# Attention's softmax sums divided out at the gate, and five element-wise steps moved between engines, in a two-layer hybrid diffusion step

## The chip, the cores and the metric

One core of a Trainium2 chip runs the whole step as one program. The metric is the device time of one execution in microseconds (us). Engines are named as in the profile: PE is TensorE's matmul (PEld its weight loads), DVE is VectorE, ACT is ScalarE, POOL is GpSimd, SP is the engine that issues most transfers.

## The reference

The model is a backbone of two layers over 640 tokens (512 latent, 128 context) of 1024 channels, in float32. Each layer normalises the tokens, projects them to 76 blocks of 128 columns (and 48 more), runs four branches on column slices of that, and merges the branches:

- RWKV-7 time mixing, in both directions, 8 heads handled as 4 pairs; at the end a group norm, a bonus term and a gate
- multi-head latent attention, 8 heads of 64 value columns, latent tokens over 640 keys, context tokens over 128
- a Mamba-2 state space branch (SSD)
- an RG-LRU: a gated linear recurrence, in both directions

The part that the change is about most is the attention, where the output is also multiplied by a gate afterwards:

```python
s = jnp.einsum('bqhd,bkhd->bhqk', qblk, k).astype(F32) * scale
p = jax.nn.softmax(s, axis=-1).astype(v.dtype)
return jnp.einsum('bhqk,bkhd->bqhd', p, v)
...
branches = jnp.stack([o_rw * jax.nn.silu(rw_gate), o_mla * jax.nn.silu(mla_gate), ...
```

and of the RG-LRU: `u = sqrt(-expm1(2 log_a)) * (g_i * xc)`, then the scan `h = a h + u` forward and backward.

## The kernel before

Activations lie with channels on the 128 partitions and the 640 tokens in the free dimension. Dense projections (`dense`, `zs`, `merge`, `output`) split both operands into a rounded part and a remainder and make three matmuls of 320 columns from each product (L246); the weights are split by an ACT cast (L233) and a DVE subtraction (L234).

The program runs a layer in stages. RWKV comes first, with projections that later stages need as background. Then two generators are woven with a background queue at fixed rates: `mla_heads` and then `mla_attend` for the attention, `lru` for the RG-LRU, and the remaining dense projections. After that SSD runs beside the merge projections, then the output projection. Generators emit instructions; a planner then orders each engine's list when the program is built, taking emission order as priority and its own costs as time, so that an instruction may stand later in an engine's list than instructions emitted after it. Each engine works its list strictly in that order.

In `mla_attend` a unit is one head and one tile of 128 queries. For a unit, `scores` makes six matmuls into a PSUM pair of banks (`pd`, two buffers; L1181), DVE takes the maximum (L1184) and scales it (L1186), ACT makes the exponentials with their row sums (`ae`, L1188), DVE takes the reciprocal of the sums (L1189) and multiplies the exponentials by it (L1190). `turn_p` transposes the result on PE in blocks of 128 (L1199: five, or one for the context tile), and copies the five blocks out of PSUM: four on ACT (L1201), the fifth on DVE (L1203), into `aPT`. The scores of the unit two later are emitted right after a unit's transposes. At a pair's second head (`e == 1`) a DVE operation on two columns (L1129) joins the two heads' copies, and the value products of both heads (L1132) go to one PSUM bank (`oT`, one buffer) that holds four token tiles; after the fourth tile and after the context tile, DVE multiplies them with the gate (L1136). Between them stand the transposes of the next heads' queries and keys (`turned`, L1081) with their splits (L1084, L1085, L239, L240).

In `lru`, for each of 4 blocks and 2 directions, DVE prepares the gates (L1458 to L1462), POOL multiplies (L1463), ACT takes a square root for both directions (L1468), POOL multiplies again (L1472), and DVE scans latent and context tokens (L1476). In `rw_end`, POOL makes the bonus term (L889) and, behind DVE's norm (L893, L894), adds it (L895); PE then transposes the sum (L541).

Of the kernel before, what the change touches and what calls it, by code (L numbers as in the profile page):

```python
# [10 lines left out]
F32 = mybir.dt.float32  # L11
# [10 lines left out]
TL, TC = 512, 128  # L22
# [147 lines left out]
class K:  # L170
# [703 lines left out]
    def rw_end(self, l, p, H, od):  # L874
# [17 lines left out]
        self.rsqrt(s2, s1, 1.0 / 64, 64e-5, p)  # L892
        tt(out=on, in0=on, in1=bc(s2), op=ALU.mult)  # L893
        tt(out=on, in0=on, in1=P["lng"][:, pr * 64:pr * 64 + 64].unsqueeze(1).broadcast_to([128, 10, 64]), op=ALU.mult)  # L894
        nc.gpsimd.tensor_tensor(out=on, in0=on, in1=q3, op=ALU.add)  # L895
        gate = p.tile([128, T], F32, name="gate", tag="rwv", bufs=1)
        nc.sync.dma_start(out=gate, in_=self.z(l, Z_RWG + pr))
        yield
# [159 lines left out]
    def mla_attend(self, l, od):  # L1058
# [37 lines left out]
        self.turn = {}  # L1096
        yield from heads((0, 1))
        todo = heads(range(2, 8))
        S = {}
        units = [(hp, t, e) for hp in range(4) for t in range(5) for e in range(2)]  # L1100
        keys = lambda t: range(5) if t < 4 else (5,)
        for i, u in enumerate(units[:2]):
            S[u] = self.scores(p, self.turn[u[2]], u[1])
            yield
        for i, (hp, t, e) in enumerate(units):
            if t == 0 and e == 0:
                gate = p.tile([128, T], F32, name="mg", tag="mg", bufs=1)
                nc.sync.dma_start(out=gate, in_=gd[hp])
            if t == 1 and e == 0:
                self.silu_sb(p, gate, "mo")  # L1110
                o32 = p.tile([128, T], F32, name="mo", tag="mo", bufs=1)
            S[hp, t, e] = self.turn_p(p, *S[hp, t, e], len(keys(t)))
            yield
            if i + 2 < len(units):
                n = units[i + 2]
                h = 2 * n[0] + n[2]
                while h not in self.turn:
                    next(todo)
                S[n] = self.scores(p, self.turn[h], n[1])
                yield  # L1120
            if next(todo, 1) is None:
                yield
            if e == 1:
                if t % 4 == 0:
                    oT = self.ps("o")
                o = oT[:, t % 4 * 128:t % 4 * 128 + 128]

                k = 511 if len(keys(t)) > 1 else 0
                nc.vector.scalar_tensor_tensor(out=S[hp, t, 0][:, 0:2], in0=S[hp, t, 1][:, k:k + 2], scalar=0.0, in1=S[hp, t, 0][:, 0:2], op0=ALU.mult, op1=ALU.add)  # L1129
                for j, kt in enumerate(keys(t)):  # L1130
                    for x in range(2):
                        nc.tensor.matmul(o[64 * x:64 * x + 64], vt[:, kt, hp * 128 + 64 * x:hp * 128 + 64 * x + 64],  # L1132
                                         S[hp, t, x][:, j * 128:j * 128 + 128], start=j == 0, stop=j == len(keys(t)) - 1)
                if t >= 3:
                    tok = slice(0, TL) if t == 3 else slice(TL, T)
                    nc.vector.tensor_tensor(out=o32[:, tok], in0=oT[:, 0:tok.stop - tok.start], in1=gate[:, tok], op=ALU.mult)  # L1136
                yield
                if t == 4:
                    nc.sync.dma_start(out=od[:, hp], in_=o32)
# [28 lines left out]
        nc.vector.tensor_tensor(out=x, in0=x, in1=cos, op=ALU.mult)  # L1168
        nc.vector.tensor_tensor(out=x, in0=x, in1=s, op=ALU.add)

    def scores(self, p, qk, t):

        nc = self.nc
        pd = self.pd()
# [11 lines left out]
        nc.vector.tensor_scalar(out=m[:, 0:1], in0=m[:, 0:1], scalar1=-scale, scalar2=None, op0=ALU.mult)  # L1186
        e = p.tile([128, 2, 320], F32, name="ae", tag="ae", bufs=2)[:, 0:len(cuts), 0:w]
        nc.scalar.activation(out=e, in_=view, func=AF.Exp, scale=scale, bias=m[:, 0:1], accum_out=m[:, 1:2])  # L1188
        nc.vector.reciprocal(out=m[:, 1:2], in_=m[:, 1:2])  # L1189
        nc.vector.tensor_scalar(out=e, in0=e, scalar1=m[:, 1:2], scalar2=None, op0=ALU.mult)  # L1190
        return pd, e

    def turn_p(self, p, pd, e, n):

        nc = self.nc
        e = e.rearrange("p a b -> p (a b)")
        PT = p.tile([128, T], F32, name="aPT", tag="aPT", bufs=3)
        for i in range(n):
            nc.tensor.transpose(pd[:, i // 4, i % 4 * 128:i % 4 * 128 + 128], e[:, i * 128:i * 128 + 128], self.c["ident"])  # L1199
        k = min(n, 4)  # L1200
        nc.scalar.copy(PT[:, 0:k * 128], pd[:, 0, 0:k * 128])  # L1201
        if n > 4:
            nc.vector.tensor_copy(PT[:, TL:T], pd[:, 1, 0:128])  # L1203
        return PT

    def conv(self, u, acc, w, b, taps):
# [200 lines left out]
    def lru(self, l, od):  # L1407
# [26 lines left out]
        for blk in range(4):  # L1434
# [6 lines left out]
            for d in range(2):  # L1441
# [18 lines left out]
                stt(out=e, in0=tr, scalar=2.0, in1=e, op0=ALU.add, op1=ALU.mult)  # L1460
                stt(out=tr, in0=t2, scalar=1.0, in1=e, op0=ALU.add, op1=ALU.mult)
                stt(out=ti, in0=ti, scalar=1.0, in1=xc, op0=ALU.add, op1=ALU.mult)  # L1462
                pt_(out=ti, in0=ti, in1=e, op=ALU.mult)  # L1463
                un.append((tr, ti, t2))
                if d == 0 and b < 4:
                    ahead = conved(*ahead)
# [2 lines left out]
            hs = []  # L1469
            for d, (tr, ti, t2) in enumerate(un):  # L1470
                i = 4 * d + blk
                pt_(out=t2, in0=t2, in1=ti, op=ALU.mult)  # L1472
                for t0, t1, init in ((0, TL, P["slru"][:, i:i + 1]), (TL, T, 0.0)):
                    s = slice(t0, t1)
                    rv = (lambda x: x[:, s]) if d == 0 else (lambda x: x[:, s][:, ::-1])
                    nc.vector.tensor_tensor_scan(rv(ti), rv(tr), rv(t2), init, ALU.mult, ALU.add)  # L1476
                nc.gpsimd.tensor_copy(fin[:, d, blk:blk + 1], ti[:, T - 1:T] if d == 0 else ti[:, TL:TL + 1])
                hs.append(ti)
                yield
# [262 lines left out]
```

## Time and profile before

| | |
|---|---|
| median of 3 runs | 2428.43 us (2424.76 to 2429.99) |
| profiled execution | 2425.01 us, its span 2423.1 us |
| PE busy | 2295.9 us, 95% |
| DVE busy | 1709.8 us, 71% |
| ACT busy | 1101.4 us, 45% |
| POOL busy | 485.1 us, 20% |
| mean granted TensorE clock | 0.974 |

A share of busy time is a mean over stages. The time of PE's records overlaps, as matmuls are pipelined, so the spacing of starts tells what one costs. The profile names for each idle stretch of an engine what ended it; the windows give busy times and the granted clock for a stretch; the timeline lists an engine's instructions in order of time.

### The profile page before, as it was taken

Reading aid. Unit: us, or ns where it says so; the run is one execution under the profiler, and the core shown is the slowest. Engines: PE = TensorE matmul, PEld = TensorE weight load, DVE = VectorE, ACT = ScalarE, POOL = GpSimd, SP = SyncE. Lnnn points to the kernel's source line nnn. Section 1 sums busy time; section 2 is a strip of 40 time slices with the busy share of each in tenths; the row PEclk is TensorE's granted clock in tenths of the full one; section 3 lists DMA queues with packets and bytes.
Section 4 is the critical chain, followed back from the end, with each engine's and each line's share of the span. In section 5 each row is a group of like instructions: output and inputs, shape, how many; then the busy total and the mean of one; then the engine's idle time right before and its main releaser. Section 6 shows DMA issues by size and latency. Waiting matters only on the chain. (4 is left out here: it accounts for less than half of the span.)

```text
span 2423.1 us, 52542 instructions
## 1 busy us (share of the span) xinstructions
PE 2295.9 (95%) x21106; PEld 2044.0 (84%) x21106; DVE 1709.8 (71%) x3831; ACT 1101.4 (45%) x2182; POOL 485.1 (20%) x645
## 2 busy tenths in 40 slices
PE   6999999999989999999999999999999988999999
PEld 4888778889988888987998979797989977898799
DVE  6684767665487878597766767777737877788973
ACT  3544344443345665562335353535224555656331
POOL 0211212231101120144012121213111013103520
PEclk9999999999999999999999999899999999999999
DMA  6553434423432213734633424141424322155354
GB/s 247 167 167 118 133 121 131 126 84 109 135 123 78 80 65 112 251 115 127 212 97 123 128 65 132 59 120 61 123 84 152 106 83 89 63 173 191 118 171 131
DMA packets 159204, 300.98 MB, mean 124 GB/s; under 512 B 59881, under 2 KB 70601, under 8 KB 158961
## 3 DMA queue, kind: packets, MB, share of 16 engines
q1 hardware_dynamic: 158528, 296.24, 37.7%
q8 instruction: 166, 2.72, 0.5%
q0 software_dynamic: 432, 1.38, 0.2%
q14 instruction: 78, 0.63, 0.1%
HBM read 221.17 MB, written 76.39 MB: 123 GB/s over the span
## 5 line engine op out<-in xcount | busy, mean ns | idle before, releaser
L246 PE MATMUL dn<-hh,whi 128*128 128x320 f32 x2368 | 765.3, 323 | 3.2 <-ACT zst L279 1.4
L246 PE MATMUL dn<-hl,whi 128*128 128x320 f32 x2368 | 745.4, 315 | 0.0
L246 PE MATMUL dn<-hh,wlo 128*128 128x320 f32 x2368 | 744.9, 315 | 0.0
L246 PEld LDWEIGHTS dn<-hh,whi 128*128 128x128 f32 x2368 | 447.8, 189 | 32.6 <-issue 6.8
L246 PEld LDWEIGHTS dn<-hl,whi 128*128 128x128 f32 x2368 | 448.7, 189 | 7.1 <-issue 1.8
L246 PEld LDWEIGHTS dn<-hh,wlo 128*128 128x128 f32 x2368 | 447.6, 189 | 6.5 <-issue 2.8
L234 DVE TENSOR_TENSOR wlo<-raw,whi 128x1024 fp32r<-128x1024 f32 (+1 forms) x184 | 240.6, 1308 | 122.3 <-ACT whi L233 119.2
L233 ACT CAST whi<-raw 128x1024 fp32r<-128x1024 f32 (+1 forms) x184 | 191.5, 1041 | 229.8 <-PE dn L246 194.9
L246 PE MATMUL dn<-omh,whi 128*128 128x320 f32 x408 | 135.7, 335 | 6.5 <-DVE mx L1541 2.9
L246 PE MATMUL dn<-oml,whi 128*128 128x320 f32 x408 | 131.4, 322 | 3.5 <-DVE oml L240 3.5
L810 POOL COPY S<-V 64x128 f32<-64x128 f32 x128 | 57.4, 448 | 382.6 <-PE ps L541 176.5
L246 PE MATMUL dn<-omh,wlo 128*128 128x320 f32 x408 | 129.2, 318 | 3.2 <-DVE wlo L234 3.2
L541 PE MATMUL ps<-Q,BK 64*64 64x192 f32 x1280 | 103.3, 342 | 13.7 <-DVE Q L673 11.2
L673 DVE TENSOR_TENSOR Q<-ps,cpack 64x384 f32<-64x384 f32 x160 | 88.8, 555 | 38.6 <-ACT W L671 34.4
L541 PEld LDWEIGHTS ps<-S,Q 128*64 128x64 f32 x1920 | 74.1, 143 | 36.1 <-issue 18.4
L281 ACT COPY zst<-dn 128x320 f32<-128x320 f32 (+1 forms) x104 | 43.9, 422 | 131.1 <-PE dn L246 90.9
L541 PE MATMUL ps<-S,Q 128*64 128x64 f32 x1920 | 90.4, 233 | 10.8 <-DVE S L855 6.5
L246 PEld LDWEIGHTS dn<-omh,whi 128*128 128x128 f32 x408 | 78.6, 194 | 25.4 <-issue 9.1
L671 ACT COPY W<-ps 64x384 f32<-64x384 f32 x160 | 75.6, 473 | 52.0 <-PE ps L541 49.5
L277 ACT ACTIVATE zst<-dn 128x320 f32<-128x320 f32 x128 | 55.5, 434 | 90.0 <-PE dn L246 60.6
L541 PEld LDWEIGHTS ps<-Q,BK 64*64 64x64 f32 x1280 | 60.3, 136 | 38.7 <-DVE Q L673 19.6
L756 DVE TENSOR_TENSOR X<-X,Lu 80x31 f32<-80x31 f32 (+15 forms) x248 | 85.5, 345 | 6.8 <-DMA X<-in_eye_dram 0.8
(575 smaller groups left out, 4837.2 us busy)
## 6 DMA issues: line engine op xcount, KB each, us to landing
raw<-in_w_in_dram SPq DMA_DIRECT2D x152, 512.0 KB
zd<-zst SPq DMA_DIRECT2D x150, 320.0 KB
raw<-in_ada_w_dram SPq DMA_DIRECT2D x48, 512.0 KB
th<-zd SPq DMA_DIRECT2D x64, 320.0 KB
raw<-in_w_branch_dram SPq DMA_DIRECT2D x32, 512.0 KB
om<-od SPq DMA_DIRECT2D x32, 320.0 KB
u<-zd SPq DMA_DIRECT2D x26, 320.0 KB
raw<-in_w_out_dram SPq DMA_DIRECT2D x16, 512.0 KB
```

The source lines that it names most:

```text
L233: nc.scalar.copy(hi[:, 0:w], raw[:, 0:w])
L234: nc.vector.tensor_tensor(out=lo[:, 0:w], in0=raw[:, 0:w], in1=hi[:, 0:w].bitcast(F32), op=ALU.subtract)
L246: self.nc.tensor.matmul(o, w[wi], x[xi][:, sl], start=first and i == 0, stop=last and i == 2)
L277: nc.scalar.activation(out=u[:, tok], in_=t, func=AF.Tanh, scale=0.5)
L281: nc.scalar.copy(u[:, tok], t)
L541: self.nc.tensor.matmul(o, x, y, start=start, stop=stop, skip_group_check=True)
L671: nc.scalar.copy(W[r, u:u + 2].rearrange("p u x t -> p (u x t)"), ps[e][r, 0:384])
L673: nc.vector.tensor_tensor(out=Q[e][o, u:u + 2].rearrange("p u x t -> p u (x t)"), in0=ps[e][o, 0:384].rearrange("p (u x) -> p u x", u=2), ...
L756: nc.vector.tensor_tensor(out=o, in0=X[0:nb, 0:m, k:k + 1].broadcast_to([nb, m, n]), in1=Lu[0:nb, k, k + 1:].unsqueeze(1).broadcast_to([nb ...
L810: nc.gpsimd.tensor_copy(S[e][o, 0:2], pairs(V[o], s))
```

## The change

In attention the exponentials are no longer multiplied by the reciprocal. The reciprocals of a pair's two heads are written to two columns of a small tile (`rs`). For each pair of units PE spreads them: one transpose of the second head's column, broadcast to 128 columns, ahead of the value products, and one of the first head's column, broadcast to 64, over the upper half behind them. They lie in the right half of the PSUM bank `oT`, which now holds two token tiles and is taken three times per head pair in place of twice. DVE multiplies the gate by the spread reciprocals and then the products by the gate, after tiles 1, 3 and 4. The copy out of `turn_p` is one ACT copy of all blocks, and the join of the two heads' copies is an ACT operation on one column in place of a DVE one on two.

In the RG-LRU the two POOL multiplies per block and direction are on DVE, and in `rw_end` the last sum is on DVE.

```diff
-        nc.gpsimd.tensor_tensor(out=on, in0=on, in1=q3, op=ALU.add)
+        tt(out=on, in0=on, in1=q3, op=ALU.add)
...
-        S = {}
+        S, r = {}, {}
...
-        for i, u in enumerate(units[:2]):
-            S[u] = self.scores(p, self.turn[u[2]], u[1])
+        def scores(hp, t, e):
+            if e == 0:
+                r[hp, t] = p.tile([128, 2], F32, name="rs", tag="ar", bufs=3)
+            S[hp, t, e] = self.scores(p, self.turn[2 * hp + e], t, r[hp, t][:, e:e + 1])
+
+        for u in units[:2]:
+            scores(*u)
...
             if e == 1:
-                if t % 4 == 0:
+                if t % 2 == 0:
                     oT = self.ps("o")
-                o = oT[:, t % 4 * 128:t % 4 * 128 + 128]
-                k = 511 if len(keys(t)) > 1 else 0
-                nc.vector.scalar_tensor_tensor(out=S[hp, t, 0][:, 0:2], in0=S[hp, t, 1][:, k:k + 2], scalar=0.0, in1=S[hp, t, 0][:, 0:2], op0=ALU.mult, op1=ALU.add)
+                o, ro = (oT[:, i + t % 2 * 128:i + t % 2 * 128 + 128] for i in (0, 256))
+                nc.tensor.transpose(ro, r[hp, t][:, 1:2].broadcast_to([128, 128]), c["ident"])
+                k = 639 if len(keys(t)) > 1 else 0
+                nc.scalar.activation(out=S[hp, t, 0][:, 0:1], in_=S[hp, t, 1][:, k:k + 1], func=AF.Identity, scale=0.0, bias=S[hp, t, 0][:, 0:1])
                 for j, kt in enumerate(keys(t)):
                     for x in range(2):
                         nc.tensor.matmul(o[64 * x:64 * x + 64], vt[:, kt, hp * 128 + 64 * x:hp * 128 + 64 * x + 64],
                                          S[hp, t, x][:, j * 128:j * 128 + 128], start=j == 0, stop=j == len(keys(t)) - 1)
-                if t >= 3:
-                    tok = slice(0, TL) if t == 3 else slice(TL, T)
-                    nc.vector.tensor_tensor(out=o32[:, tok], in0=oT[:, 0:tok.stop - tok.start], in1=gate[:, tok], op=ALU.mult)
+                nc.tensor.transpose(ro[0:64], r[hp, t][:, 0:1].broadcast_to([128, 64]), c["ident"])
+                if t % 2 or t == 4:
+                    n = 256 if t < 4 else 128
+                    tok = slice((t + 1) * 128 - n, (t + 1) * 128)
+                    nc.vector.tensor_tensor(out=gate[:, tok], in0=oT[:, 256:256 + n], in1=gate[:, tok], op=ALU.mult)
+                    nc.vector.tensor_tensor(out=o32[:, tok], in0=oT[:, 0:n], in1=gate[:, tok], op=ALU.mult)
...
-        nc.vector.reciprocal(out=m[:, 1:2], in_=m[:, 1:2])
-        nc.vector.tensor_scalar(out=e, in0=e, scalar1=m[:, 1:2], scalar2=None, op0=ALU.mult)
+        nc.vector.reciprocal(out=r, in_=m[:, 1:2])
...
-        k = min(n, 4)
-        nc.scalar.copy(PT[:, 0:k * 128], pd[:, 0, 0:k * 128])
-        if n > 4:
-            nc.vector.tensor_copy(PT[:, TL:T], pd[:, 1, 0:128])
+        nc.scalar.copy(PT[:, 0:n * 128], pd.rearrange("p a b -> p (a b)")[:, 0:n * 128])
...
-                pt_(out=ti, in0=ti, in1=e, op=ALU.mult)
+                tt(out=ti, in0=ti, in1=e, op=ALU.mult)
...
-                pt_(out=t2, in0=t2, in1=ti, op=ALU.mult)
+                tt(out=t2, in0=t2, in1=ti, op=ALU.mult)
```

## Rows read from the trace of the kernel before

**Rows 1.** The page's first part: engine, busy us, share of the span, instructions.
```profile
PE 2295.9 (95%) x21106; PEld 2044.0 (84%) x21106; DVE 1709.8 (71%) x3831; ACT 1101.4 (45%) x2182; POOL 485.1 (20%) x645
```

**Rows 2.** Windows, attention's stretches: length, then busy us by engine, granted clock, DMA.
```profile
780.00:980.00 200.00, 186.14 (x1371) 164.93 (x1370) 164.32 (x375) 124.70 (x241) 33.18 (x25) 0.97 0.29 92
...
1960.00:2172.00 212.00, 196.50 (x1428) 174.74 (x1428) 169.05 (x380) 128.27 (x247) 37.81 (x27) 0.96 0.29 95
```

**Rows 3.** PE's waits, whole span: who waited for whom, total us, times, longest us.
```profile
PE pd L1199 <- DVE ae L1190: 18.5, 11, 4.7
...
PE ps L1081 <- DVE qTl L1085: 6.7, 5, 2.1
...
PE ps L1132 <- DVE aPT L1129: 4.4, 2, 4.1
...
PE ps L541 <- POOL on L895: 2.0, 1, 2.0
```

**Rows 4.** Timeline of DVE: start us, us, instruction, idle time before it and its end.
```profile
862.15 2.59 DVE L1476 TENSOR_TENSOR_SCAN lt<-lt,pcol,l 128x512 f32<-128x512 f32 x1 [1.71 <-POOL l L1472]
...
2044.69 0.15 DVE L1186 TENSOR_SCALAR m<-m 128x1 f32<-128x1 f32 x1
2047.97 2.55 DVE L1476 TENSOR_TENSOR_SCAN lt<-lt,pcol,l 128x512 f32<-128x512 f32 x1 [3.12 <-POOL l L1472]
...
2050.76 1.25 DVE L1476 TENSOR_TENSOR_SCAN lt<-lt,pcol,l 128x512 f32<-128x512 f32 x1
...
2052.25 0.13 DVE L1189 RECIPROCAL m<-m 128x1 f32<-128x1 f32 x1
...
2093.41 2.57 DVE L1476 TENSOR_TENSOR_SCAN lt<-lt,pcol,l 128x512 f32<-128x512 f32 x1 [0.90 <-POOL l L1472]
```

**Rows 5.** Timeline of ACT, same stretch.
```profile
2047.53 0.80 ACT L1188 ACTIVATE ae<-pd,m 128x640 f32<-128x640 f32 x1
...
2048.31 0.58 ACT L1201 COPY aPT<-pd 128x512 f32<-128x512 f32 x1
```

**Rows 6.** Timeline of PE, same stretch.
```profile
2048.00 0.31 PE L246 MATMUL dn<-hl,whi 128*128 128x320 f32 x1
2048.14 0.31 PE L246 MATMUL dn<-hh,wlo 128*128 128x320 f32 x1
2053.12 0.87 PE L1199 MATMUL pd<-cpack,ae 128*128 128x128 f32 x3 [4.66 <-DVE ae L1190]
...
2054.05 0.47 PE L1181 MATMUL pd<-kTl,qTh 96*128 96x320 f32 x1
2054.32 0.47 PE L1181 MATMUL pd<-kTh,qTl 96*128 96x320 f32 x1
```

**Rows 7.** DVE's groups by line and form: count, busy us, mean ns, idle before.
```profile
L234 DVE TENSOR_TENSOR wlo<-raw,whi 128x1024 fp32r<-128x1024 f32 x182 | 239.5, 1316 | 121.3 <-ACT whi L233 118.2 <-ACT xs L833 1.9 <-DMA cv<-lx 0.4
...
L1190 DVE TENSOR_SCALAR ae<-ae,m 128x640 f32<-128x640 f32 x64 | 41.2, 644 | 1.1
...
L1203 DVE COPY aPT<-pd 128x128 f32<-128x128 f32 x64 | 18.1, 284 | 14.1 <-ACT aPT L1201 13.6
...
L1345 DVE TENSOR_TENSOR yo<-pd,ea 128x256 f32<-128x256 f32 x40 | 15.0, 410 | 1.9 <-PE pd L1341 1.9
...
L1544 DVE TENSOR_TENSOR y<-y,mx 128x640 f32<-128x640 f32 x16 | 13.1, 819 | 0.1
```

**Rows 8.** Timeline of PE at five transposes of the SSD stage.
```profile
1021.00 0.71 PE L1237 MATMUL pd<-cpack,cu 128*128 128x128 f32 x5
1021.63 0.49 PE L1289 MATMUL pd<-bc,bc 64*128 64x128 f32 x4
```

**Rows 9.** DVE's waits, whole span.
```profile
DVE m L1189 <- ACT ae L1188: 12.4, 18, 1.1
```

**Rows 10.** POOL at a head pair's end: a timeline row; line L895's durations min/median/max.
```profile
331.91 1.26 POOL L889 TENSOR_TENSOR gnq<-V,bon 128x640 f32<-128x640 f32 x1 [30.44 <-DVE s L888]
...
L895 POOL TENSOR_TENSOR on<-on,gnq x8: 1530/1584/2620, 337.0 to 1817.2; 128x640 f32<-128x640 f32 x8
```

More of the change, by code (lines that the diff above doesn't have):

```diff
@@ L1118, in mla_attend @@
                     next(todo)
-                S[n] = self.scores(p, self.turn[h], n[1])
+                scores(*n)
                 yield
@@ L1169, in rope, with scores @@
         nc.vector.tensor_tensor(out=x, in0=x, in1=s, op=ALU.add)
-    def scores(self, p, qk, t):
+    def scores(self, p, qk, t, r):
         nc = self.nc
```

## The prediction

> **What bounds the kernel now.** I read the page's busy shares first: PE is busy for 2295.9 us, 95% of a span of 2423.1 us [rows 1]. So the kernel is bound by TensorE's list, and only two things can shorten it: less work on PE, or less idle time and slow clock on PE. What the change takes from DVE, ACT or GpSimd counts only where PE waits for it.
>
> Next came the windows of the two stretches in which attention runs beside RG-LRU and the dense background [rows 2]. In 780 to 980 us PE is idle for 200 - 186.14 = 13.9 us, in 1960 to 2172 us for 212 - 196.50 = 15.5 us. The granted clock is 0.97 and 0.96 there. So attention holds 29.4 us of idle time and some clock.
>
> Third, who PE waits for [rows 3]. The largest wait after the start is that of the probability transposes (L1199) for DVE's normalising multiply of the exponentials (L1190): 18.5 us in 11 waits. The wait of the value products (L1132) for DVE's joining operation (L1129) is 4.4 us. The head transposes (L1081) wait 6.7 us for the splits of the turned heads (L1085). At the RWKV head pair's end there is 2.0 us behind the GpSimd sum (L895).
>
> Last, one of the long waits, in time. DVE finishes a unit's scaled maximum at 2044.84; its next work is two pairs of RG-LRU scans, the first after 3.12 us idle for GpSimd's product, and only at 2052.25 comes that unit's reciprocal and then the multiply [rows 4]. The exponentials had been ready since 2048.33 [rows 5]. PE had nothing left at 2048.45 and started the transposes at 2053.12, after 4.66 us idle [rows 6]. So DVE's queue makes the wait, not the exponential. The code emits maximum, reciprocal and multiply together; that scans stand between them is the planner's order.
>
> The clock follows these gaps. Behind this one the score products start 0.27 us apart, where dense products of the same 320 columns started 0.14 to 0.15 us apart before it [rows 6]: the 1.2 GHz level instead of 2.4.
>
> **Part by part.** *Sums taken up at the gate.* Removed from DVE: 64 multiplies of 640 columns, 41.2 us, 64 copies, 18.1 us [rows 7], 16 smaller multiplies and 40 two-column joins. Added: per head pair five products of a PSUM operand with the gate in place of one (two of 256 columns at t = 1, two at t = 3, two of 128 at t = 4, less the old two); at 0.41 us for 256 columns [rows 7] that is under 8 x 1.3 = 10 us on DVE. DVE stays well below PE in total.
>
> PE is what pays: two transposes for each of 40 pairs of units (2 layers, 4 head pairs, 5 token tiles), 80 in all. Five transposes of 128 columns in a row fill 1021.00 to 1021.63, when the next product starts [rows 8]: 0.126 us each, and 0.11 between their own starts ((0.71 - 0.27)/4). Nothing covers them, since PE is the bound: 80 x 0.126 = 10 us (bounds: 80 x 0.11 = 9, and double, 20, if all stood at the low clock).
>
> A transpose's record is 0.27 us long (the first gap of the 0.71 us of five at 0.11 [rows 8]), which is more than its share of the queue because records overlap. The Trainium skill ("TensorE: Matmul & The Clock Gate", Part 4: PE-mode transpose) gives about 275 ns for one in a kernel's context; the record agrees, but charged in full the 80 would be 22 us and the sum 2421. The spacing of the row decides.
>
> What goes from PE's waits: the 18.5 us for the multiply, as the transposes then need the exponential alone; 4.4 for the join, as one ACT copy takes both halves: 22.9 us. Where it waits next: the exponential was over 4.8 us before the transposes in the example [rows 5, 6].
>
> ACT gets the copy of 640 instead of 512 columns (0.58 us for 512 [rows 5], so about 0.15 more) and a join of one column (not in the trace: between nothing and that 0.58; I take 0.25, as it is nearer to the small end). On the path of a pair this replaces DVE's copy (0.28 [rows 7]) and its join: 0.40 against 0.28 and the join, so nothing. Queued behind the join are the next exponentials; ACT is busy for 124.70 of 200 us [rows 2], which covers it. Without cover, 40 x 0.4 = 16 us of ACT time would show.
>
> A new wait: the first of the two transposes needs the second unit's reciprocal, still on DVE. Behind it in PE's list stand the pair's value products and all dense work. Cost from 0, as DVE's reciprocal came straight after the exponential in 18 of 80 cases [rows 9], to the whole of a burst of scans.
>
> *RG-LRU products on DVE.* GpSimd loses 32 products, of some 1.58 us each by the sum's row [rows 10]. DVE gains 32 x 0.82 us (same form, two SBUF operands, L1544 [rows 7]) = 26 us, less than the 41.2 + 18.1 that it loses above. The scan no longer waits for GpSimd, 3.12 us in the example, and the first scan, beside GpSimd's second product, took 2.55 us where the next took 1.25 [rows 4].
>
> The Trainium skill ("SBUF — State Buffer", Who interferes with whom) has DVE operations with two SBUF inputs contend with GpSimd ones that read SBUF, the later one blocking until the first ends. By that the moved products spare DVE the doubled scans; the trace agrees (2.55 against 1.25).
>
> In the example the scans took DVE from 2047.97 to 2052.25 [rows 4]. With both scans at 1.25 and two products more, such a burst is 4.28 - 1.30 + 2 x 0.82 = 4.6 us. It can still delay a maximum or a reciprocal. A stretch of this kind, its first scan at twice the length, stands four times beside attention, first at 862.15, last at 2093.41 [rows 4]; half a burst each time, 4 x 2.5 = 10 us, is what I let come back (bounds 0 and the whole 22.9).
>
> *The sum at the head pair's end.* Eight sums: GpSimd took 1.53 to 2.62 us each [rows 10], DVE takes 0.82. PE's wait of 2.0 [rows 3] goes. The sum now waits on DVE for GpSimd's product (L889), over at 333.17, where the first sum began at 337.0 [rows 10]; behind it on DVE stand a state chain's copies, 0.82 us later than before in the worst case: 8 x 0.82 = 6.6 us on the other side. I take the 2.0 alone.
>
> *Clock and the rest of the queue.* (1 - 0.97) x 200 x 2 + (1 - 0.96) x 212 x 2 = 29 us run at the low level [rows 2]. Some 8 of them I take to lie in the gaps themselves; in the other 21 a product takes 0.27 instead of 0.15, so 21 x (1 - 0.147/0.266) = 9.4 us are lost. Nearly all follow a removed wait: I take 8. Of the head transposes' 6.7 us I take 3 for a shorter DVE queue (bounds 0 and 6.7).
>
> **Sum**, on the profiled execution (2425.0, its span 2423.1 and 1.9 around it; the median of the three runs is 3.4 higher): 2425.0 + 10 (transposes) - 22.9 (attention's waits) - 2.0 (the sum) - 8 (clock) - 3 (head transposes) + 10 (come back) = 2409 us.
>
> **Rivals.**
> *A, nothing comes back.* The exponential is always early, as in the example, and the bursts are short enough. 2425 + 10 - 24.9 - 9.4 - 6.7 = 2394. For it: no scan waits for GpSimd any more. Against: a maximum stays on DVE ahead of each exponential, behind the same bursts.
> *B, the wait moves to the exponential.* The planner puts the transposes as soon as it believes them ready; today that is behind the multiply, then behind the exponential. A burst that stood between maximum and reciprocal stands ahead of the maximum and delays it as much; the 18.5 us and the clock stay. 2425 + 10 - 4.4 - 2.0 = 2428.6. Against: the chain to be delayed is two DVE operations shorter, and a unit's scores run two units ahead.
> *C, slower: the reciprocal holds PE at the divisor's transpose.* Between a second unit's probability transposes and the divisor's stand 5 x 0.11 + 6 x 0.147 = 1.4 us of PE work. If DVE reaches the reciprocal later than that after the exponential, PE waits, 40 times. Behind a weight split (L234, 1.3 us) and one operation like L1544 (0.82) [rows 7] it is 2.1 - 1.4 = 0.7 us each, 28 us, more than the 24.9 saved: 2425 + 10 - 24.9 + 28 = 2438, clock as now. It decides from (24.9 - 10)/40 = 0.37 us each. Against: the 18 of 80 cases without any queue [rows 9].
>
> **How the numbers follow.** Forecast (2400 to 2418) 0.47; A (2385 to 2400) 0.17; B (2419 to 2433) 0.21; C (2434 to 2446) 0.15. The point is the forecast's, 2409. Range 2389 to 2434: it leaves out most of C and the lower part of A, 0.2 in all. A measurement of this kernel can tell about 0.2% from no change, so the bounds are 2423.6 and 2433.3 around the median 2428.4: faster 0.47 + 0.17 + a quarter of B = 0.69; same the rest of B = 0.16; slower 0.15.
>
> **What would show it.** Right: the probability transposes wait for DVE nowhere; DVE scans all near 1.25 us; idle PE in the two stretches down from 29 to some 13 us; granted clock there 0.98 or more; 80 new transposes about 0.12 us apart. A: idle under 8 us. B: the transposes wait for ACT's exponential by some 18 us. C: the new transposes wait for the reciprocal. I would be wrong altogether if PE's idle time outside attention moved by more than 10 us, since the planner orders the whole program anew and I have priced that at nothing.

## The result and the profile after

The changed kernel takes 2394.38 us (median of 4 runs, 2391.97 to 2397.69) where the kernel before, beside it, takes 2427.64: a ratio of 0.9863, 95% interval 0.9848 to 0.9879, or 33 us less. Its profiled execution took 2396.4 us, 28.6 less than that of before; its span is 2394.6, 28.5 less. The forecast, worked out for the profiled execution, was 16 less (2409).

The page's first part of the kernel after stands against [rows 1]:

```profile
PE 2299.2 (96%) x21186; PEld 2042.0 (85%) x21186; DVE 1661.3 (69%) x3719; ACT 1118.2 (47%) x2222; POOL 423.5 (18%) x605
```

PE has 80 instructions more and 3.3 us more of busy time, in a span 28.5 us shorter. So nothing was taken off PE: the gain is idle time, and time at the low clock, that went. DVE lost 48.5 us and GpSimd 61.6; by themselves they count for nothing.

Where it went is read by stages. Windows of the kernel before (length, busy us of PE, PEld, DVE, ACT, POOL, granted clock, DMA share, GB/s): the two stretches from attention's first transposes to SSD's first ones, where attention, RG-LRU and background are woven, and then the two RWKV stages:

```profile
709.60:1012.70 303.10, 283.60 (x1965) 254.68 (x1966) 228.95 (x541) 171.96 (x320) 45.80 (x34) 0.97 0.33 108
1891.10:2187.30 296.20, 275.92 (x1927) 247.29 (x1926) 227.84 (x539) 168.56 (x316) 46.82 (x34) 0.97 0.31 104
90.20:709.60 619.40, 596.40 (x6686) 518.36 (x6685) 402.88 (x992) 256.05 (x528) 120.18 (x226) 0.98 0.40 126
1299.70:1891.10 591.40, 566.84 (x6259) 507.68 (x6258) 403.88 (x957) 248.66 (x510) 116.54 (x227) 0.97 0.33 102
```

The same four of the kernel after, then the two stretches of it that answer to [rows 2]:

```profile
712.40:1006.70 294.30, 286.30 (x2005) 254.58 (x2006) 204.34 (x481) 179.59 (x340) 21.48 (x18) 0.98 0.33 111
1882.50:2162.70 280.20, 276.03 (x1977) 246.29 (x1976) 207.14 (x480) 176.74 (x337) 20.00 (x18) 1.00 0.34 114
91.60:712.40 620.80, 600.26 (x6686) 521.48 (x6685) 404.46 (x996) 256.62 (x528) 115.24 (x222) 0.98 0.39 125
1295.70:1882.50 586.80, 563.70 (x6257) 505.46 (x6257) 403.73 (x960) 248.57 (x510) 111.20 (x223) 0.97 0.33 103
...
777.00:955.00 178.00, 172.56 (x1285) 147.79 (x1284) 138.44 (x310) 129.15 (x257) 19.64 (x16) 0.98 0.28 93
1949.00:2136.00 187.00, 184.80 (x1395) 161.61 (x1394) 142.66 (x310) 131.69 (x263) 18.81 (x16) 1.00 0.30 99
```

The attention stages went from 303.1 + 296.2 = 599.3 us to 574.5: 24.8 of the span's 28.5 us. The two RWKV stages together lost 3.2. In the last two rows PE is idle for 5.4 and 2.2 us, 7.6 together where [rows 2] had 29.4. Below, "the attention stages" are these two together. Their "idle" is the sum of PE's gaps that end in them; it is 5.6 us more than length less PE's busy time in the rows, as the gap ahead of their very first transposes counts. Their "low clock" is the time at 1.2 GHz. Before: 45.4 us idle, 38.3 us low clock. After: 17.8 and 13.5.

PE's waits in the kernel after, whole span (who waited for whom: total us, times, longest), against [rows 3]:

```profile
PE ps L541 <- DVE Q L673: 15.1, 24, 2.9
PE ps L541 <- DVE un L846: 7.4, 13, 1.0
...
PE ps L1457 <- ACT lt L1458: 3.9, 1, 3.9
...
PE ps L1081 <- DVE qTl L1085: 2.7, 2, 1.4
...
PE pd L1210 <- ACT ae L1200: 2.1, 2, 1.7
...
PE ps L541 <- DVE on L895: 0.7, 2, 0.3
```

The 18.5 us of the probability transposes (now L1210) for DVE and the 4.4 of the value products are gone; what is left of the former is 2.1 for the exponential. The RWKV sum's 2.0 for POOL is 0.7 for DVE. Read alone, this says that taking the multiply out of the chain did it. The experiments say that most of it came by other parts of the change.

DVE's timeline of the kernel after, at a burst of scans, against [rows 4] (start us, us, instruction, idle before it):

```profile
2025.32 0.15 DVE L1198 TENSOR_SCALAR m<-m 128x1 f32<-128x1 f32 x1
2026.49 1.56 DVE L1480 TENSOR_TENSOR l<-l,lt 128x640 f32<-128x640 f32 x2 [1.02 <-ACT l L1476]
2027.96 1.28 DVE L1484 TENSOR_TENSOR_SCAN lt<-lt,pcol,l 128x512 f32<-128x512 f32 x1
2029.16 0.40 DVE L1484 TENSOR_TENSOR_SCAN lt<-lt,l 128x128 f32<-128x128 f32 x1
2029.48 0.14 DVE L1201 RECIPROCAL rs<-m 128x1 f32<-128x1 f32 x1
2029.53 1.26 DVE L1484 TENSOR_TENSOR_SCAN lt<-lt,pcol,l 128x512 f32<-128x512 f32 x1
2030.71 0.40 DVE L1484 TENSOR_TENSOR_SCAN lt<-lt,l 128x128 f32<-128x128 f32 x1
2031.03 0.80 DVE L1196 TENSOR_REDUCE m<-pd 128x1 f32<-128x640 f32 x1
2031.74 1.87 DVE L1159 SCALAR_TENSOR_TENSOR lu<-sth,lu 128x640 f32<-128x640 f32 x1
2033.54 0.14 DVE L1198 TENSOR_SCALAR m<-m 128x1 f32<-128x1 f32 x1
```

The second product of each direction (L1480, 1.56 us for both) stands on DVE, the first scan takes 1.28 us where it took 2.55, and the wait ahead of the burst is 1.02 for ACT's root instead of 3.12 for GpSimd. PE's timeline of the kernel after, same stretch:

```profile
2027.47 0.31 PE L246 MATMUL dn<-hh,wlo 128*128 128x320 f32 x1
2027.62 0.27 PE L1135 MATMUL ps<-cpack,rs 128*128 128x128 f32 x1
2027.64 0.39 PE L246 MATMUL dn<-hh,whi 128*128 128x320 f32 x1
2027.87 0.31 PE L246 MATMUL dn<-hl,whi 128*128 128x320 f32 x1
...
2028.76 0.72 PE L1210 MATMUL pd<-cpack,ae 128*128 128x128 f32 x5
...
2034.71 0.77 PE L1210 MATMUL pd<-cpack,ae 128*128 128x128 f32 x5 [1.74 <-ACT ae L1200]
```

A new transpose (L1135) stands between dense products: from 2027.47 to 2027.87 three instructions take 0.40 us, where two products at 0.147 take 0.29, so the transpose costs about 0.11. The gap at 2034.71 is a maximum that stood behind the scans: L1196 at 2031.03 in the rows above, then its scaling (L1198), the exponential, and PE. Between maximum and scaling stands another RG-LRU step, L1159, with 1.87 us; it takes 0.80 to 0.81 in six of its eight places, and here GpSimd's sum of both directions (L1490) ran beside it from 2031.38 to 2032.93. So the longest wait for the exponential that is left has a GpSimd operation in it, too.

### The profile page after: what moved, and what is told of

Same layout as the page of the kernel before. It is cut to its first block, busy times and chain, and to the rows that moved or that the text cites. A ratio compares the mean times of both kernels' runs of the same rounds, so it can differ in the third digit from the quotient of the medians.

```text
span 2394.6 us, 52515 instructions
## 1 busy us (share of the span) xinstructions
PE 2299.2 (96%) x21186; PEld 2042.0 (85%) x21186; DVE 1661.3 (69%) x3719; ACT 1118.2 (47%) x2222; POOL 423.5 (18%) x605
## 5 line engine op out<-in xcount | busy, mean ns | idle before, releaser
L234 DVE TENSOR_TENSOR wlo<-raw,whi 128x1024 fp32r<-128x1024 f32 (+1 forms) x184 | 235.8, 1282 | 134.1 <-ACT whi L233 128.1
L541 PE MATMUL ps<-Q,BK 64*64 64x192 f32 x1280 | 103.8, 341 | 17.5 <-DVE Q L673 15.1
L673 DVE TENSOR_TENSOR Q<-ps,cpack 64x384 f32<-64x384 f32 x160 | 88.8, 555 | 36.2 <-ACT W L671 32.0
L541 PEld LDWEIGHTS ps<-S,Q 128*64 128x64 f32 x1920 | 73.2, 141 | 30.8 <-issue 22.1
```

The costliest lines, as they stand in the source:

```text
L234: nc.vector.tensor_tensor(out=lo[:, 0:w], in0=raw[:, 0:w], in1=hi[:, 0:w].bitcast(F32), op=ALU.subtract)
L541: self.nc.tensor.matmul(o, x, y, start=start, stop=stop, skip_group_check=True)
L673: nc.vector.tensor_tensor(out=Q[e][o, u:u + 2].rearrange("p u x t -> p u (x t)"), in0=ps[e][o, 0:384].rearrange("p (u x) -> p u x", u=2), ...
```

## The experiments

Each ratio is to the kernel before on the same chip, with its 95% interval. Diffs are against the kernel before unless said otherwise.

**The three parts alone.** Theory 1: the multiply's place in DVE's chain makes the wait, so attention's part alone brings most of the gain. Its rival: what stands in front of reciprocal and multiply in DVE's queue makes it, so the RG-LRU products bring it. The planner orders PE's list in the attention stages anew in every variant that changes attention or RG-LRU, and no run held that order fixed, so a part of each such ratio may be the order's.

`attn_only`, the changed kernel with GpSimd's three steps left on GpSimd:

```diff
-                tt(out=ti, in0=ti, in1=e, op=ALU.mult)
+                pt_(out=ti, in0=ti, in1=e, op=ALU.mult)
...
-                tt(out=t2, in0=t2, in1=ti, op=ALU.mult)
+                pt_(out=t2, in0=t2, in1=ti, op=ALU.mult)
...
-        tt(out=on, in0=on, in1=q3, op=ALU.add)
+        nc.gpsimd.tensor_tensor(out=on, in0=on, in1=q3, op=ALU.add)
```

> Attention's part alone; the RG-LRU products and the head pair's sum are on GpSimd again. Theory 1 (the multiply in DVE's queue made PE wait; taking it out of the chain is what pays): most of the 33 us stays, 2398 to 2406, and the probability transposes wait for nothing on DVE. Theory 2 (GpSimd's products in front of and beside the scans made the long bursts, and these would hold the maximum as well): no more than a third stays, 2416 to 2425, and PE waits for the exponential instead, by over 10 us.

Measured: 0.9972 [0.9957, 0.9987], some 7 us of the 33; the attention stages take 594.4 us, 35.1 of them idle. PE's waits in this kernel:

```profile
PE ps L1081 <- DVE qTl L1085: 8.4, 4, 2.8
...
PE ps L1081 <- DVE m L1198: 4.5, 2, 2.3
...
PE ps L1135 <- DVE m L1198: 3.1, 1, 3.1
...
PE pd L1210 <- ACT ae L1200: 2.0, 2, 1.6
```

and DVE's timeline in it at the burst of [rows 4]:

```profile
2046.99 0.42 DVE L1148 TENSOR_TENSOR mo<-ps,mg 128x256 f32<-128x256 f32 x1
2049.62 2.57 DVE L1484 TENSOR_TENSOR_SCAN lt<-lt,pcol,l 128x512 f32<-128x512 f32 x1 [2.21 <-POOL l L1480]
...
2053.93 0.13 DVE L1201 RECIPROCAL rs<-m 128x1 f32<-128x1 f32 x1
2053.99 0.80 DVE L1196 TENSOR_REDUCE m<-pd 128x1 f32<-128x640 f32 x1
```

The wait for the multiply is gone, but the burst is as before, 2.21 us of standing and 2.57 of a doubled scan, and now a maximum stands behind it at 2053.99. PE waits instead for the head transposes' splits and for maxima (8.4 + 4.5 + 3.1 us, where before had 6.7 + 3.3 + 0 in these three). The 3.1 us are named after a scaled maximum that ended at 906.92 us; a reciprocal ended 0.05 us earlier, behind the same burst, so either may have released PE. For the exponential itself PE waits 2.0 us (L1210), not over 10 as the expectation's second theory had it. So the waits moved to other users of DVE's queue, not to the exponential. They moved in part: idle time fell by 10.3 us and low clock from 38.3 to 21.0, yet the stages are only 4.9 us shorter, because PE's time without its gaps rose from 599.3 - 45.4 = 553.9 to 594.4 - 35.1 = 559.3, with 80 new transposes in it. The small gain has two causes, then, waits that moved and work that PE got.

`lru_only`, both RG-LRU products on DVE and nothing else:

```diff
-                pt_(out=ti, in0=ti, in1=e, op=ALU.mult)
+                tt(out=ti, in0=ti, in1=e, op=ALU.mult)
...
-                pt_(out=t2, in0=t2, in1=ti, op=ALU.mult)
+                tt(out=t2, in0=t2, in1=ti, op=ALU.mult)
```

> The RG-LRU's 32 products alone on DVE, attention as before. Theory 1: the multiply still stands behind a burst of some 4.6 us, so the 18.5 us of PE's wait fall by a third at most: 2418 to 2426. Theory 2: without the wait for GpSimd and the doubled scans the multiply comes in time: 2402 to 2412, and the wait for the multiply is under 6 us.

Measured: 0.9929 [0.9909, 0.9949], 17 us; stages 583.3, idle 30.8. PE's waits:

```profile
PE ps L1449 <- ACT lt L1450: 7.7, 4, 3.3
...
PE ps L1081 <- DVE qTl L1085: 3.6, 6, 1.4
...
PE pd L1199 <- DVE ae L1190: 2.7, 6, 0.6
```

With reciprocal and multiply where they were, the 18.5 us wait for the multiply falls to 2.7. A new one of 7.7 stands at the RG-LRU gates. The time lies 2 us above the rival's range and the wait inside it. Theory 1, that attention's part alone brings most, falls with this pair of runs; that the burst ahead of the multiply made its wait holds.

`rwend_only`, the sum at the RWKV head pair's end on DVE:

```diff
-        nc.gpsimd.tensor_tensor(out=on, in0=on, in1=q3, op=ALU.add)
+        tt(out=on, in0=on, in1=q3, op=ALU.add)
```

> The sum at the RWKV head pair's end alone on DVE. By the forecast's term PE's 2.0 us wait goes and nothing else changes: 2425 to 2427. Rival (the planner's new order around it and the DVE queue behind it count for more): anything from -6 to +6 us, 2421 to 2434, with PE's waits for DVE in RWKV (Q, un, S) changed by over 3 us.

Measured: 0.9962 [0.9949, 0.9975], 9 us where the forecast had 2. The wait for the multiply is unchanged at 18.5. The three parts multiply to 0.9972 x 0.9929 x 0.9962 = 0.9863, the ratio of the whole, so they hardly work on one another.

**The chain tested inside the changed kernel.** `mul_back` puts a multiply by 1.0 of the exponentials back behind the reciprocal; `chain_back` puts the multiply by the reciprocal itself back, and spreads ones in its place (against the kernel after):

```diff
         nc.vector.reciprocal(out=r, in_=m[:, 1:2])
+        nc.vector.tensor_scalar(out=e, in0=e, scalar1=1.0, scalar2=None, op0=ALU.mult)
```

> The changed kernel with a multiply by 1.0 of the exponentials on DVE between exponential and transposes: the DVE step is back in the chain, all else as changed. Theory 1: PE waits for it again, 12 us or more with the clock behind them: 2408 to 2420. Theory 2 (the chain does not matter once GpSimd is out of the bursts): 2394 to 2399.

```diff
-                nc.tensor.transpose(ro, r[hp, t][:, 1:2].broadcast_to([128, 128]), c["ident"])
+                nc.tensor.transpose(ro, c["ones"][:, 0:1].broadcast_to([128, 128]), c["ident"])
...
-                nc.tensor.transpose(ro[0:64], r[hp, t][:, 0:1].broadcast_to([128, 64]), c["ident"])
+                nc.tensor.transpose(ro[0:64], c["ones"][:, 0:1].broadcast_to([128, 64]), c["ident"])
...
+        nc.vector.tensor_scalar(out=e, in0=e, scalar1=r, scalar2=None, op0=ALU.mult)
```

> The changed kernel with the multiply of the exponentials by the reciprocal back on DVE ahead of the transposes (both DVE steps in the chain as before); the spread columns are ones, so PE's and the gate's work is as changed. Theory 1: 8 us or more over the whole change, with 8 us or more of PE's wait for the multiply. Theory 2 (with GpSimd out of the bursts the chain has slack): 0 to 4 us over it.

Measured: 0.9868 [0.9848, 0.9888] and 0.9860 [0.9838, 0.9882], against 0.9863 without. The transposes again wait for DVE's multiply, 4.8 and 5.8 us, and the stages' idle time is 24.3 and 25.1 us against 17.8, yet the time doesn't tell them from the changed kernel. In their profiled executions the stages take 578.9 and 579.4 us against 574.5, but the kernel before, `rwend_only` and `rw_skip`, whose instructions PE starts in the same order in these stages, take 599.3, 602.7 and 602.8, so 3 to 4 us of one execution can be chance and these 4 to 5 hardly stand out. Once the burst ahead of it is short, the multiply costs less than these runs can separate, some 0.2%.

**Without attention's part, and which product.** `no_attn` is the kernel before with both RG-LRU products and the RWKV sum on DVE; `lru_second` has on DVE only the product that feeds the scan. First `no_attn`:

```diff
-        nc.gpsimd.tensor_tensor(out=on, in0=on, in1=q3, op=ALU.add)
+        tt(out=on, in0=on, in1=q3, op=ALU.add)
...
-                pt_(out=ti, in0=ti, in1=e, op=ALU.mult)
+                tt(out=ti, in0=ti, in1=e, op=ALU.mult)
...
-                pt_(out=t2, in0=t2, in1=ti, op=ALU.mult)
+                tt(out=t2, in0=t2, in1=ti, op=ALU.mult)
```

> The kernel before with the RG-LRU products and the head pair's sum on DVE, attention's part left out. If the parts add up as measured one by one (0.9929 x 0.9962): ratio 0.989, some 26 us under before, 7 over the whole change. If attention's part needs the others to pay (its waits only show once the bursts are short): 0.992 or more, that is 14 us or more over the whole change.

and `lru_second`:

```diff
-                pt_(out=t2, in0=t2, in1=ti, op=ALU.mult)
+                tt(out=t2, in0=t2, in1=ti, op=ALU.mult)
```

> The kernel before with only the second RG-LRU product (the scan's input) on DVE; the first stays on GpSimd. Theory 2a (the scan's wait for GpSimd and its doubled length beside the other direction's product make the long bursts): most of the 17 us of both products, 12 us or more under before, and PE's wait for the multiply falls from 18.5 us to under 8. Theory 2b (the first product, which holds up the normalising multiply beside it, makes as much): 5 to 11 us under before, with 8 us or more of that wait left.

Measured: `no_attn` 0.9900 [0.9878, 0.9922], so 1.0 of the 1.37% needs nothing of attention; its wait for the multiply is 3.3 us. `lru_second` 0.9924 [0.9911, 0.9938], the same as both products. Its wait, and below it DVE's group of scans in it:

```profile
PE pd L1199 <- DVE ae L1190: 5.0, 8, 1.0
...
L1476 DVE TENSOR_TENSOR_SCAN lt<-lt,pcol,l 128x512 f32<-128x512 f32 x16 | 20.4, 1274 | 0.1
```

and the same group of the kernel before (busy us, mean ns, then idle time ahead of it):

```profile
L1476 DVE TENSOR_TENSOR_SCAN lt<-lt,pcol,l 128x512 f32<-128x512 f32 x16 | 25.5, 1596 | 14.1 <-POOL l L1472 14.1
```

The moved product takes 14.1 us of standing and 5.1 us of lengthened scans out of DVE's queue and puts 16 x 0.78 = 12.5 us of its own in. The first scan at four places ran beside GpSimd's product of the other direction and took twice as long [rows 4]; no scan does now. The first product (L1463) adds nothing that shows.

**What the rest of attention's part is worth.** `copy_on_act` is `no_attn` with the copy of all blocks and the join on ACT, the division left in DVE's chain, and no new transposes; `copy_only` moves the copy and leaves the join on DVE:

```diff
-        k = min(n, 4)
-        nc.scalar.copy(PT[:, 0:k * 128], pd[:, 0, 0:k * 128])
-        if n > 4:
-            nc.vector.tensor_copy(PT[:, TL:T], pd[:, 1, 0:128])
+        nc.scalar.copy(PT[:, 0:n * 128], pd.rearrange("p a b -> p (a b)")[:, 0:n * 128])
```

> RG-LRU products and the head pair's sum on DVE, and of attention's part only the copy of all blocks on ACT; join and multiply on DVE. The kernel with copy and join on ACT was 18 us under the one with neither (2386.8 against 2404.6). Theory 3a (the copy pays, as it frees the pair of PSUM banks for the next scores without DVE): within 4 us of copy and join, 2385 to 2391. Theory 3b (the join pays, as the value products waited for it behind DVE's queue): within 5 us of neither, 2399 to 2409.

and in `copy_on_act` the join as well:

```diff
-                k = 511 if len(keys(t)) > 1 else 0
-                nc.vector.scalar_tensor_tensor(out=S[hp, t, 0][:, 0:2], in0=S[hp, t, 1][:, k:k + 2], scalar=0.0, in1=S[hp, t, 0][:, 0:2], op0=ALU.mult, op1=ALU.add)
+                k = 639 if len(keys(t)) > 1 else 0
+                nc.scalar.activation(out=S[hp, t, 0][:, 0:1], in_=S[hp, t, 1][:, k:k + 1], func=AF.Identity, scale=0.0, bias=S[hp, t, 0][:, 0:1])
```

> The same kernel plus, of attention's part, only the copy of all blocks and the join on ACT; sums are divided out on DVE in the chain as before, so there are no new transposes. Theory 3 (of attention's part the copy and the join pay, the multiply's place does not): 5 to 12 us under the kernel without attention's part, and no slower than the whole change. Theory 1 (the multiply's place pays): within 3 us of the kernel without attention's part.

Measured: `copy_on_act` 0.9819 [0.9799, 0.9839], 2386.8 us, the fastest of all and below the changed kernel with no overlap of the intervals; `copy_only` 0.9868 [0.9845, 0.9891]. So on top of `no_attn` the copy brings some 0.3% (its interval overlaps), the join another 0.5%, and the division at the gate, 0.9863 against 0.9819, costs 0.44%, about 10.7 us. Copy and join together are 18 us under `no_attn`, more than the 5 to 12 expected. At which wait the join pays isn't shown: PE waited 2.0 us for it in `copy_only` (L1132) and 1.0 in `copy_on_act`, while the wait for the multiply fell from 7.6 to 4.1. The page's first line and PE's waits of `copy_on_act`:

```profile
PE 2285.6 (96%) x21106; PEld 2033.0 (85%) x21106; DVE 1689.6 (71%) x3767; ACT 1117.9 (47%) x2222; POOL 421.2 (18%) x605
...
PE pd L1199 <- DVE ae L1190: 4.1, 7, 1.7
...
PE ps L1132 <- ACT aPT L1129: 1.0, 1, 1.0
```

PE still waits 4.1 us for the multiply, and its stages are idle for 21.1 us against the changed kernel's 17.8; but PE is busy for 13.6 us less. The changed kernel buys 3 us of idle time with 80 PE instructions.

**What these 80 cost.** `twice_T` issues each new transpose twice (against the kernel after):

```diff
                 nc.tensor.transpose(ro, r[hp, t][:, 1:2].broadcast_to([128, 128]), c["ident"])
+                nc.tensor.transpose(ro, r[hp, t][:, 1:2].broadcast_to([128, 128]), c["ident"])
...
                 nc.tensor.transpose(ro[0:64], r[hp, t][:, 0:1].broadcast_to([128, 64]), c["ident"])
+                nc.tensor.transpose(ro[0:64], r[hp, t][:, 0:1].broadcast_to([128, 64]), c["ident"])
```

> The changed kernel with each of the 80 transposes of the sums issued twice: the price of the transposes by itself. By the spacing of the row, 0.126 us each: 10 us over the whole change (9 to 12). By the length of the record, 0.27 us each: 22 us. If PE's remaining idle time swallowed them: under 4 us.

Measured: 0.9874 [0.9852, 0.9895], 2401.2 us. The intervals overlap. The two ratios lie 2.7 us apart, which excludes the 22 us of the record's length, but doesn't tell 7 us from none. In the traces, though, the attention stages take 581.5 against 574.5 us at the same idle time (17.4 against 17.8) and low clock (12.5 against 13.5): 7.0 us for 80, 0.09 each, by one execution of either kernel. The other 3 to 4 us of the division's price weren't isolated.

**The RWKV sum.** `rw_skip` leaves the sum out altogether, so that RWKV's output lacks its bonus:

```diff
-        nc.gpsimd.tensor_tensor(out=on, in0=on, in1=q3, op=ALU.add)
```

> The kernel before without the sum at the RWKV head pair's end (the bonus is left out of RWKV's output). The sum on DVE was 9 us under before, where 2 were forecast. If the wait for GpSimd's sum and its place beside DVE are what pays: as much as on DVE or a little more, 8 to 13 us under before. If the order that the planner makes anew is what pays: not tied to that, 0 to 5 us under before or above it.

Measured: 0.9948 [0.9935, 0.9960], against 0.9962 with the sum on DVE. By these ratios GpSimd's sum cost some 12.6 us and DVE's costs 3 of them; the intervals of the two overlap. The planner's order isn't what pays in `rw_skip`: by the starts in the traces, 16 of PE's 21106 instructions stand at another place than before. Part of the mechanism stands in the timelines of the kernel before, DVE first, then POOL:

```profile
337.01 1.22 DVE L234 TENSOR_TENSOR wlo<-raw,whi 128x1024 fp32r<-128x1024 f32 x1
338.14 2.02 DVE L718 TENSOR_TENSOR_SCAN cs<-m,e 128x260 f32<-128x260 f32 x1
...
1525.77 1.99 DVE L718 TENSOR_TENSOR_SCAN cs<-m,e 128x260 f32<-128x260 f32 x1
...
337.04 2.58 POOL L895 TENSOR_TENSOR on<-on,gnq 128x640 f32<-128x640 f32 x1 [3.87 <-DVE on L894]
...
1525.67 1.53 POOL L895 TENSOR_TENSOR on<-on,gnq 128x640 f32<-128x640 f32 x1 [3.87 <-DVE on L894]
```

In these rows, of two operations side by side the one that begins later gets longer. At 1525.67 the sum begins first and takes its usual 1.53 us, and the scan 0.10 us behind it takes 1.99 where others of the kind take some 0.7. At 337.01 DVE's weight subtraction (L234) begins first and takes its usual 1.22; the sum, 0.03 us behind it, takes 2.58, and the scan behind the sum 2.02. Three of the 16 scans are lengthened so. The group of these scans, kernel before and then `rwend_only`:

```profile
L718 DVE TENSOR_TENSOR_SCAN cs<-m,e 128x260 f32<-128x260 f32 x16 | 15.2, 949 | 1.1
```

```profile
L718 DVE TENSOR_TENSOR_SCAN cs<-m,e 128x260 f32<-128x260 f32 x16 | 11.3, 704 | 1.0
```

So DVE gets back 3.9 us of scans for the 8 x 0.82 = 6.6 that it takes on. The Trainium skill ("SBUF — State Buffer", Who interferes with whom) has DVE and GpSimd share a port pair under an exclusive lock; these rows agree in that the operation that began first kept its usual 1.53 or 1.22 us and the other one paid. Where PE gains the 9 us is shown in part: in the profiled execution of `rw_skip` the RWKV stages take 1203.0 us where they took 1210.8, with 41.3 us of idle time against 47.6. In `rwend_only` the 2.0 for POOL fell to 0.7 for DVE, while the waits for Q (L673) and un (L846) rose from 11.2 and 5.1 to 15.7 and 7.4 (15.1 and 7.4 in the changed kernel) and that for S (L855) fell from 6.5 to 1.5. Its profiled execution was among its longest and shows no gain at all.

**More of the same.** `copy_lru_all` is `copy_on_act` with the RG-LRU's two other GpSimd steps on DVE too:

```diff
-            pt_(out=hs[0], in0=hs[0], in1=hs[1], op=ALU.add)
+            tt(out=hs[0], in0=hs[0], in1=hs[1], op=ALU.add)
...
-            pt_(out=hs[0], in0=hs[0], in1=g, op=ALU.mult)
+            tt(out=hs[0], in0=hs[0], in1=g, op=ALU.mult)
```

> Copy and join on ACT, products and sum on DVE, and also the RG-LRU's last two GpSimd operations per block (the sum of both directions and the product with the gate) on DVE. Theory 2 (GpSimd work beside DVE lengthens DVE's bursts): 2 to 8 us under the kernel with copy and join on ACT, that is 2379 to 2385. Rival (these two stand where nobody waits, and DVE gets 16 x 0.82 us more): 0 to 4 us over it.

Measured: 0.9835 [0.9822, 0.9849], no better than `copy_on_act`. These two steps stand behind the scans, not ahead of them. The lengthened L1159 is gone with them (0.80 to 0.82 us in all eight places, where `copy_on_act` has 1.50 and 1.88 in two), and in the profiled execution the attention stages take 563.8 us against 567.3; why the whole is no faster isn't shown. So relieving GpSimd as such brought no gain beyond `copy_on_act`.

## Why the prediction was right in sign and short in size

**The bound and the stage were right.** PE's list bounds the kernel, and the attention stages hold 24.8 of the 28.5 us. The time lies in the range, 15 us below the point (13 by the profiled execution) and on rival A's 2394. The signs are A's as well: in the two stretches PE is idle for 7.6 us, where the forecast had 13 and A under 8. The other signs came as written: the probability transposes wait for DVE nowhere, no scan of this form takes over 1.29 us, the granted clock is 0.98 and 1.00. A had 0.17 of the chances. That its number was met so closely is luck in part: it had the sum at 2 us and copy and join at nothing, and by what follows both were worth more.

**Attention's waits, -22.9: the size was right, the credit misplaced.** Both waits went. But the prediction had read in [rows 4] and [rows 5] that DVE's queue made the wait, not the exponential, and still credited its end to taking the multiply out of the chain alone. That ends the wait by its name, with the bursts as they were (`attn_only`), but part of it comes back elsewhere. `lru_second` ends most of it (18.5 to 5.0) with the multiply in place; `mul_back` and `chain_back` put the multiply back at no price that the times show. The step that failed is "what goes from PE's waits": a wait named after the last operation of a queue was booked on that operation, and what stood ahead of it was booked as a mere help under the RG-LRU's part. The Trainium skill ("Perfetto Trace Analysis", Tensor Engine Instruction) has DVE as a strict FIFO; the rows of `attn_only` agree, where the same burst with its 2.21 us of standing moved PE's wait to other users of DVE.

**Rival B was near in time for attention alone, and wrong about the wait.** Its 2428.6 supposed that a burst delays the maximum as much as it had delayed the multiply, so that PE waits some 18.5 us for the exponential. With the bursts unchanged the time is nearly that of before (`attn_only`, 0.9972), but PE waits 2.0 us for the exponential: a part of the waits moved to other users of DVE, and the new transposes took part of what was saved. With the bursts shortened the exponential's wait is 2.1.

**What comes back, +10: too much.** 2.1 us for the exponential (L1210) and 3.9 at the RG-LRU gate (L1457) are the new waits in the changed kernel, 6.0 in all, and the 1.7 of them at 2034.71 have a lengthened DVE step behind them that the prediction had no term for (L1159). The burst was forecast at 4.6 us; in the row it is 1.56 + 1.28 + 0.40 + 0.14 + 1.26 + 0.40, less overlaps 2031.03 - 2026.49 = 4.5. The length was right; half of one at four places was too dear.

**The transposes, +10: near.** 7.0 us by `twice_T`, 0.09 each instead of 0.126, by one execution of either kernel; the whole division costs 10.7 by the ratios. The spacing was the right row to take, not the record of 0.27. On DVE the gate's products are four more per head pair, six in place of two, where the prediction has "five products" in place of one; it has no part in the sum.

**Clock, -8.** Low clock in the attention stages fell from 38.3 to 13.5 us. At 1 - 0.147/0.266 = 0.45 of it lost the 24.8 us less are worth up to 11; some of it lies in the gaps, which are counted already. It fell with the gaps, as forecast, though not in step with them from run to run: `lru_only` has less idle time than `attn_only` (30.8 against 35.1) and more low clock (34.8 against 21.0).

**Head transposes, -3: too little.** The wait for qTl fell from 6.7 to 2.7; with those for a maximum and kTl at the same line, the total went from 6.7 + 3.3 + 2.8 = 12.8 to 2.7 + 0.7 + 0.2 = 3.6. A shorter DVE queue pays at every user of DVE, and only one of them was priced.

**The sum, -2: too little.** 9 us by `rwend_only`, with the term itself (2.0 of wait) right as far as it went. The prediction priced what PE waited for at that instruction, and not what GpSimd's sum did to the scans beside it, although [rows 10] showed the same sum once at 1.53 and once at 2.62 us. The planner's new order can't be the reason in `rw_skip`, which keeps PE's order but for 16 instructions; how the rest divides between the clock and DVE's shorter queue stays open. In the changed kernel's own profiled execution the RWKV stages lost 3.2 us.

**Join and copy on ACT, 0 on the path: missed.** They were priced at 0.40 us of ACT against 0.28 and the join on DVE, so nothing. Per piece that was close: the kernel after's rows are

```profile
L1211 ACT COPY aPT<-pd 128x640 f32<-128x640 f32 x64 | 43.9, 692 | 23.7 <-PE pd L1210 23.1 <-ACT aPT L1211 0.3
...
L1138 ACT ACTIVATE aPT<-aPT 128x1 f32<-128x1 f32 x40 | 11.8, 296 | 0.4
```

0.69 and 0.30 us, where 0.73 and 0.25 were taken. On top of `no_attn` they bring 0.8%, the division at the gate takes 0.44% back. So their place counts, not their length. A reason that fits, but wasn't tested by itself, is that these steps no longer stand in DVE's queue behind scans and weight splits (in the row of 187 us ACT is busy for 131.69 us and DVE for 142.66). So the part that gave the change its shape is its one loss.

**Rival C, the reciprocal holding PE.** Out: ahead of all 40 of the second head's transposes (L1135) PE stood for 0.3 us in the kernel after, and that for its own work, not for DVE. In `attn_only`, with the old bursts, one wait of 3.1 us at L1135, behind a burst and the reciprocal that followed it, may be the mechanism, at a single place, not forty.

**PE idle outside attention** was to move by less than 10 us. In the RWKV rows it went from (619.4 - 596.40) + (591.4 - 566.84) = 47.6 to 43.6 and their time by 3.2. The planner went over the whole program, but in these stages PE starts nearly all of its instructions in the order of before.

## What to carry to other kernels

A wait that the profile names after one instruction belongs to that instruction's queue: list what the engine did from the end of its last useful step to that instruction, and first remove what *stands* there (an operation waiting for a slower engine, or doubled beside one) before rebuilding the algorithm around the one that is named. On a kernel bound by TensorE's list, a few microseconds of TensorE work cost about their spacing, while moving a small step from the engine whose queue makes the waits to another costs little: here `copy_on_act`, which leaves the division where it was and moves only five element-wise steps, beats both kernels at 2386.8 us. And price a moved step by its neighbours as well as by itself: what ran beside it, what stood behind it.

## What the runs showed of the hardware

- Of a DVE and a GpSimd operation side by side, the one that began later got longer and the other kept its time: the 128x512 scan took 2.55 to 2.59 us against 1.25 to 1.28, the 128x260 scan 1.99, begun 0.10 us behind GpSimd's sum of 1.53, against a mean of 0.70 without that sum, and GpSimd's 128x640 sum 2.58, begun 0.03 us behind a DVE subtraction of 1.22.
- An added PE transpose of 128 columns, record 0.27 us, cost about 0.09 us among dense products (7.0 us for 80, one execution of either kernel), near its spacing of 0.11 in a row of five [rows 8].
- An ACT operation on a single column takes 0.296 us (L1138), close to half of a copy of 640 columns (0.692).
- Executions of one kernel lay up to some 10 us around their median, so the profiled execution of a part worth 9 us (`rwend_only`) showed none of it: parts of this size were told by repeated timing, and their place by traces only where a wait moved as well.
